# Lower parts of the first weights on VectorE, and the row of ln_mix kept in two accumulators

## The chip, the core and the metric

One core of one Trainium2 chip runs the kernel. The metric is the device time of one execution in microseconds (us), the median of several. TensorE (PE in the rows) multiplies and transposes, VectorE (DVE), ScalarE (ACT) and GpSimd (POOL) work element by element, and the SP queue issues all the transfers between HBM and the on-chip memory SBUF. TensorE writes its results into accumulators (PSUM), which DVE and ACT can read.

## The reference, cut to what matters

The kernel computes one inference step of a decoder layer for 1024 prompt tokens and 32 sample tokens. The change lies in its first lines, the norm of the input and the first columns of the projection:

```
def rmsnorm(x, g):
    xf = x.astype(jnp.float32)
    y = xf * lax.rsqrt(jnp.mean(xf * xf, axis=-1, keepdims=True) + EPS)
    return (y * g.astype(jnp.float32)).astype(x.dtype)
...
    a = rmsnorm(h, ln_mix)
    proj = a @ w_in
    x_m, z_m, o_m, i_pre, f_pre, x_s, z_s = jnp.split(proj, SPLIT_IDX, axis=-1)
```

`h` has 1056 rows of 1024, `ln_mix` is a vector of 1024 and `w_in` is 1024 by 2568. What follows (an S5 scan over `x_s`, a chunkwise mLSTM over `x_m`, output projections, a gated embedding and a last norm) is untouched.

## The kernel before

Every fp32 product is made of three fp32r products: an operand is split into an upper part (`hi`, a cast by ACT) and a lower part (`lo`, the operand minus `hi`), and `mm3` (L122 to L125) multiplies hi by hi, hi by lo and lo by hi. `wtile` (L97 to L117) loads a weight tile, casts `hi` on ACT (L115) and subtracts on the engine that `lo_engine[0]` names (L116). That engine is GpSimd (`G`) for the first six weight tiles: `o00` and `o01` (two halves of the first 264 output-gate columns, `o_w`), and `xs0` to `xs3` (the four 128-column tiles of x_s, `xs_w`). From L932 on it is VectorE for all later ones.

The input comes in nine row tiles of 128 rows, the last of 32 (`x_load`; five buffers). `x_tile(i)` (L151 to L179) normalises one: ACT squares and sums the row (L157; for tile 0 in two halves, L164), DVE and GpSimd make the reciprocal root (L55 and L56; `rsqrt`, the power is GpSimd's), DVE multiplies the row by it and by `ln_row` into `xn` (L159; for tile 0 in two halves, L170), TensorE transposes `xn` in two halves of four blocks (L176, accumulators `tpx`), ACT casts each half into `aTh` (L178) and DVE subtracts for `aTl` (L179). `ln_row` is the vector `ln_mix` repeated on 128 partitions: TensorE multiplies a row of ones by it (L311, two halves, accumulators `tpl`), and DVE copies both halves into SBUF (L312).

The loop at L313 takes tile after tile: load of a tile four ahead, `x_tile`, `o_tile` (24 products of the tile with the output-gate weights, L123 to L125, into `ps_o`; its evacuation is L232 on ACT and L239 on DVE), and after tiles 1, 4 and 8 the x_s columns of a chunk of tiles (`s5_x`, products into `ps_xs`, evacuation L283). Then come the x_s columns of the three other weight tiles, then the S5 stage (its transposes `tpW` on TensorE start at 97.9 us of the span), the mLSTM stage (its transposes `tpxc` from 257.2 us, `tph` to 408.8 us) and the output stages.

The order on each engine up to L933 is made by a scheduler from the program text, data dependences and `tc.high_priority()` blocks; the PE order of the S5 and mLSTM stages is written by hand. Each engine and the SP queue executes its own order strictly, and waits on semaphores. At most eight transfers are under way on the SP queue at a time: there are eight semaphores, and a transfer's issue waits for the landing of the one eight places ahead of it.

Some transposes of small constants stand among the products of the row tiles; one is `tpv` (L920), which needs `scr`, the 24 rows of `state_conv`. `tpc` (L336) needs the small `rows` transfers.

Of the kernel before, what the change touches and what calls it, by code (L numbers as in the profile page):

```python
# [8 lines left out]
F32 = mybir.dt.float32  # L9
# [20 lines left out]
def tile_hymba(ctx: ExitStack, tc: tile.TileContext, d: dict, o: list):  # L30
# [4 lines left out]
    def dma(out, in_):  # L35
        nc.sync.dma_start(out, in_)  # L36
# [46 lines left out]
    def pv(shape, name):  # L83
        return psS.tile(shape, F32, tag="sm", name=name)
# [31 lines left out]
            lo_engine[0].tensor_tensor(lo, raw, hi.bitcast(F32), op=SUB)  # L116
        return hi, lo  # L117

    lo_engine = [G]
    last_mm = [None]  # L120

    def mm3(ps, wh, wl, xh, xl, first, last):  # L122
# [11 lines left out]
    s5c = s5x.enter_context(tc.tile_pool(name="s5c", bufs=1, side="right", reuse_waits="tile"))  # L134
    xphase = ExitStack()
    xp = xphase.enter_context(tc.tile_pool(name="xp", bufs=1, side="right", reuse_waits="tile"))
    ln_row = xp.tile([128, 1024], F32, name="ln_row")

    def x_src(i):
        if i < 8:  # L140
# [3 lines left out]
    def x_load(i):  # L144
        xt = xp.tile([128, 1024], F32, tag="xt", name="xt", bufs=5)
        for q in range(1 if i else 2):
            w = 1024 if i else 512
            dma(xt[:128 if i < 8 else 32, w * q:w * q + w], x_src(i)[:, w * q:w * q + w])
        return xt

    def x_tile(i, xt):  # L151
        n = 128 if i < 8 else 32
        xn = xp.tile([128, 1024], F32, tag="xn", name="xn", bufs=4)
        ss = xp.tile([128, 1], F32, tag="ss", name="ss", bufs=3)
        rr = xp.tile([128, 2], F32, tag="rr", name="rr", bufs=3)
        if i:
            A.activation(xn[:n], xt[:n], AF.Square, accum_out=ss[:n])  # L157
            rsqrt(rr[:n, 1:2], ss[:n], 1.0 / 1024, EPS, rr[:n, 0:1])
            V.scalar_tensor_tensor(xn[:n], xt[:n], rr[:n, 1:2], ln_row[:n], op0=MUL, op1=MUL)  # L159
        else:  # L160

            s2 = xp.tile([128, 2], F32, name="s2")
            for q in range(2):
                A.activation(xn[:, 512 * q:512 * q + 512], xt[:, 512 * q:512 * q + 512], AF.Square,  # L164
                             accum_out=s2[:, q:q + 1])
            V.tensor_scalar(ss, s2[:, 0:1], 1.0 / 1024, EPS, op0=MUL, op1=ADD)
            V.scalar_tensor_tensor(rr[:, 0:1], s2[:, 1:2], 1.0 / 1024, ss, op0=MUL, op1=ADD)
            G.tensor_tensor(rr[:, 1:2], rr[:, 0:1], mhalf[:, 0:1], op=ALU.pow)
            for q in range(2):
                V.scalar_tensor_tensor(xn[:, 512 * q:512 * q + 512], xt[:, 512 * q:512 * q + 512], rr[:, 1:2],  # L170
                                       ln_row[:, 512 * q:512 * q + 512], op0=MUL, op1=MUL)
        c, off = LOC[i]
        for q in range(2):
            tp = pv([128, 4, 128], "tpx")
            for k in range(4):
                T.transpose(tp[:, k, :n], xn[:n, (4 * q + k) * 128:(4 * q + k + 1) * 128], ident[:n, :n])  # L176
            hi = aTh[c][:, 4 * q:4 * q + 4, off:off + n]
            A.copy(hi, tp[:, :, :n])  # L178
            V.tensor_tensor(aTl[c][:, 4 * q:4 * q + 4, off:off + n], tp[:, :, :n], hi.bitcast(F32), op=SUB)  # L179
# [115 lines left out]
    ow = []  # L295
    one_p = xp.tile([1, 128], F32, tag="xn", name="one_p", bufs=4)
    V.memset(one_p, 1.0)
    xts.append(x_load(0))
    ln1 = xp.tile([1, 1024], F32, tag="xn", name="ln1", bufs=4)
    dma(ln1, bcast(d["ln_mix"], 1024, 1))  # L300
    ow.append(o_w(0, 0))
    xts.append(x_load(1))
    ow.append(o_w(0, 1))
# [2 lines left out]
    dma(bgr[:, 0:4], bcast(d["b_igate"], 4))  # L306
    dma(bgr[:, 4:8], bcast(d["b_fgate"], 4))
    xts.append(x_load(3))
    for q in range(2):
        ps = pv([128, 512], "tpl")  # L310
        T.matmul(ps, one_p, ln1[:, 512 * q:512 * q + 512], start=True, stop=True)  # L311
        V.tensor_copy(ln_row[:, 512 * q:512 * q + 512], ps)  # L312
    for i in range(9):  # L313
        if i + 4 < 9:
            xts.append(x_load(i + 4))
# [1360 lines left out]
```

## Time and profile before

| what | value |
|---|---|
| device time, median of 3 runs | 655.43 us (653.66 to 656.03) |
| the profiled execution, its own time | 654.02 us |
| its span, first to last instruction | 652.3 us |
| TensorE busy | 611.8 us, 94% of the span |
| VectorE busy | 456.9 us, 70% |
| ScalarE busy | 255.3 us, 39% |
| GpSimd busy | 102.2 us, 16% |

The span is one execution; what lies around it (654.02 minus 652.3) is 1.7 us. The engines' shares are means over stages with different limits, so what a change to the first stage is worth has to be read from the rows of that stage and of those that take over its results.

### The profile page before, as it was taken

The numbers are of one execution on the slowest core, as the hardware profiler recorded it, in microseconds if no ns is written. First come the engines' busy times: TensorE is split into PE (matmuls) and PEld (weight loads), VectorE is DVE, ScalarE is ACT, GpSimd is POOL, SyncE is SP. The second block draws the span as 40 slices with busy tenths as digits, with TensorE's granted clock in tenths as the row PEclk, the third lists the DMA queues.
The fourth block names the chain that finished last, engine by engine and source line by source line (L and its number), as shares of the span: only waits on it lengthen the run. The fifth ranks groups of instructions, "written<-read, shape, count | busy, mean of one in ns | idle before, by whom it ended". The sixth has DMA issues, their size and how long they took to land.

```text
span 652.3 us, 11603 instructions
## 1 busy us (share of the span) xinstructions
PE 611.8 (94%) x4072; PEld 536.5 (82%) x4072; DVE 456.9 (70%) x1377; ACT 255.3 (39%) x630; POOL 102.2 (16%) x125
## 2 busy tenths in 40 slices
PE   5999999999999997988989897899999999999995
PEld 3999998999999986877968796777888777788885
DVE  5788969999999954998767889964222325566435
ACT  5653743333334555442232335444113225433332
POOL 6840200000000000020201123333001113111001
PEclk9999999999999998997999998999999999999999
DMA  8813353555544438362634655687342274412111
GB/s 265 244 50 56 97 160 95 132 147 156 151 116 111 112 84 275 99 209 88 171 109 114 201 151 164 205 258 219 106 130 86 76 245 141 150 57 98 64 65 65
DMA packets 112417, 90.02 MB, mean 138 GB/s; under 512 B 34080, under 2 KB 94900, under 8 KB 112360
## 3 DMA queue, kind: packets, MB, share of 16 engines
q1 hardware_dynamic: 112360, 89.29, 46.0%
q8 instruction: 32, 0.52, 0.3%
q14 instruction: 25, 0.20, 0.1%
HBM read 61.68 MB, written 27.58 MB: 137 GB/s over the span
## 4 chain that ended last, share of the span: by engine, by line
PE 66%; DMA 12%; DVE 11%; issue 4%; SPq 3%; ACT 2%; POOL 1%; POOLq 0%; DVEq 0%; ACTq 0%
PE po L1495 5%; PE po L1496 5%; PE po L1497 5%; PE po L1604 4%; PE po L1605 4%; PE po L1606 4%; DMA nmb<-d_row 3%; SPq L36 3%; PE ps_xs L123 2%; PE ps_o L123 2%; PE ps_xs L124 2%; PE ps_xs L125 2%; PE ps_o L124 2%; PE ps_o L125 2%; PE ps_xm L123 2%
## 5 line engine op out<-in xcount | busy, mean ns | idle before, releaser
L1604 PE MATMUL po<-wgh,hTh 128*128 128x512 f32 (+1 forms) x136 | 52.1, 383 | 0.0
L1606 PE MATMUL po<-wgh,hTl 128*128 128x512 f32 (+1 forms) x136 | 51.5, 379 | 0.0
L1605 PE MATMUL po<-wgl,hTh 128*128 128x512 f32 (+1 forms) x136 | 51.4, 378 | 0.0
L123 PE MATMUL ps_o<-hi_o,aTh 128*128 128x264 f32 (+2 forms) x136 | 41.0, 301 | 0.0
L123 PE MATMUL ps_zs<-aTh,hi_zs 128*128 128x256 f32 (+2 forms) x96 | 39.9, 415 | 0.0
L125 PE MATMUL ps_o<-hi_o,aTl 128*128 128x264 f32 (+2 forms) x136 | 39.4, 290 | 0.0
L124 PE MATMUL ps_o<-lo_o,aTh 128*128 128x264 f32 (+2 forms) x136 | 39.2, 289 | 0.0
L123 PE MATMUL ps_xm<-aTh,hi_xm 128*128 128x256 f32 (+2 forms) x96 | 34.7, 361 | 0.0
L1299 POOL TENSOR_TENSOR svm<-sv,bmask 96x258 fp32r<-96x258 f32 x16 | 10.1, 633 | 146.5 <-ACT xc L1088 65.9
L1495 PE MATMUL po<-woh,mh 128*128 128x512 f32 x80 | 32.6, 407 | 0.0
L1504 DVE TENSOR_TENSOR hTl<-tr,hTh 128x512 fp32r<-128x512 f32 x16 | 11.1, 691 | 30.6 <-ACT hTh L1503 30.6
L123 PE MATMUL ps_zm<-aTh,hi_zm 128*128 128x256 f32 (+2 forms) x96 | 32.0, 333 | 0.0
L1496 PE MATMUL po<-wol,mh 128*128 128x512 f32 x80 | 31.9, 399 | 0.0
L123 PE MATMUL ps_xs<-aTh,hi_xs 128*128 128x256 f32 (+2 forms) x96 | 31.4, 327 | 0.4 <-ACT xs L287 0.4
L1497 PE MATMUL po<-woh,mlo 128*128 128x512 f32 x80 | 31.7, 396 | 0.0
L125 PE MATMUL ps_zs<-aTh,lo_zs 128*128 128x256 f32 (+2 forms) x96 | 31.6, 329 | 0.0
L124 PE MATMUL ps_zs<-aTl,hi_zs 128*128 128x256 f32 (+2 forms) x96 | 31.5, 328 | 0.0
L124 PE MATMUL ps_xm<-aTl,hi_xm 128*128 128x256 f32 (+2 forms) x96 | 31.3, 326 | 0.0
L125 PE MATMUL ps_xs<-aTh,lo_xs 128*128 128x256 f32 (+2 forms) x96 | 31.3, 326 | 0.0
L124 PE MATMUL ps_xs<-aTl,hi_xs 128*128 128x256 f32 (+2 forms) x96 | 31.3, 326 | 0.0
L125 PE MATMUL ps_xm<-aTh,lo_xm 128*128 128x256 f32 (+2 forms) x96 | 31.2, 325 | 0.0
L125 PE MATMUL ps_zm<-aTh,lo_zm 128*128 128x256 f32 (+2 forms) x96 | 31.0, 323 | 0.0
(594 smaller groups left out, 1907.7 us busy)
## 6 DMA issues: line engine op xcount, KB each, us to landing
xt<-in_x_prompt SPq DMA_DIRECT2D x15, 512.0 KB
Wraw<-in_w_out SPq DMA_DIRECT2D x16, 256.0 KB
Wraw<-in_w_ple_gate SPq DMA_DIRECT2D x16, 256.0 KB
d_h<-xt SPq DMA_DIRECT2D x8, 512.0 KB
h_t<-d_h SPq DMA_DIRECT2D x8, 512.0 KB
out<-g_t SPq DMA_DIRECT2D x14, 256.0 KB
mt<-d_m SPq DMA_DIRECT2D x10, 256.0 KB
d_us<-xs SPq DMA_DIRECT2D x32, 72.0 KB
```

The costliest lines, as they stand in the source:

```text
L36: nc.sync.dma_start(out, in_)
L123: T.matmul(ps, wh, xh, start=first, stop=False)
L124: T.matmul(ps, wh, xl, start=False, stop=False)
L125: last_mm[0] = T.matmul(ps, wl, xh, start=False, stop=last).ins
L1299: G.tensor_tensor(vm[:, :nb], v3.bitcast(F32).unsqueeze(1).to_broadcast([96, nb, 129]), bmask[:, b0:b0 + nb].unsqueeze(2).to_broadcast([96 ...
L1495: T.matmul(ps, mh[:, k % 4, :], hi, start=k == 4, stop=False)
L1496: T.matmul(ps, mh[:, k % 4, :], lo, start=False, stop=False)
L1497: T.matmul(ps, mlo[:, k % 4, :], hi, start=False, stop=k == 3)
L1504: V.tensor_tensor(hTl[i][:, 4 * q:4 * q + 4, :], tp, hi.bitcast(F32), op=SUB)
L1604: T.matmul(ps[:, :b - a], hTh[i][:, k, :], hi[:, ws], start=k == 4, stop=False)
L1605: T.matmul(ps[:, :b - a], hTh[i][:, k, :], lo[:, ws], start=False, stop=False)
L1606: T.matmul(ps[:, :b - a], hTl[i][:, k, :], hi[:, ws], start=False, stop=k == 3)
```

## The change

The lower parts of the first six weight tiles are made by VectorE. The row of `ln_mix` is not copied to SBUF: the two accumulators stay, in another pool (`pn`, two banks that nothing else uses before the S5 stage's `py`, L658, at 115.9 us), and `xn` is made in halves for every tile, each half reading one accumulator. For tile 0 these two instructions have high priority. The load of `ln_mix` is written ahead of that of tile 0.

```
-    lo_engine = [G]
+    lo_engine = [V]
...
-    ln_row = xp.tile([128, 1024], F32, name="ln_row")
...
-            V.scalar_tensor_tensor(xn[:n], xt[:n], rr[:n, 1:2], ln_row[:n], op0=MUL, op1=MUL)
+            for q in range(2):
+                cs = slice(512 * q, 512 * q + 512)
+                V.scalar_tensor_tensor(xn[:n, cs], xt[:n, cs], rr[:n, 1:2], ln_row[q][:n], op0=MUL, op1=MUL)
...
-            for q in range(2):
-                V.scalar_tensor_tensor(xn[:, 512 * q:512 * q + 512], xt[:, 512 * q:512 * q + 512], rr[:, 1:2],
-                                       ln_row[:, 512 * q:512 * q + 512], op0=MUL, op1=MUL)
+            with tc.high_priority():
+                for q in range(2):
+                    V.scalar_tensor_tensor(xn[:, 512 * q:512 * q + 512], xt[:, 512 * q:512 * q + 512], rr[:, 1:2],
+                                           ln_row[q], op0=MUL, op1=MUL)
...
-    xts.append(x_load(0))
     ln1 = xp.tile([1, 1024], F32, tag="xn", name="ln1", bufs=4)
     dma(ln1, bcast(d["ln_mix"], 1024, 1))
+    xts.append(x_load(0))
...
+    ln_row = [pn([128, 512], "tpl") for _ in range(2)]
     for q in range(2):
-        ps = pv([128, 512], "tpl")
-        T.matmul(ps, one_p, ln1[:, 512 * q:512 * q + 512], start=True, stop=True)
-        V.tensor_copy(ln_row[:, 512 * q:512 * q + 512], ps)
+        T.matmul(ln_row[q], one_p, ln1[:, 512 * q:512 * q + 512], start=True, stop=True)
```

Behind these lines the scheduler orders the engines anew. In the rows below, lines of the changed kernel stand one to three higher than those of before (L172 is the tile-0 product of before's L170, L160 is L159, L181 is L179, L922 is L920).

On VectorE, from the end of tile 0's root on, there stood:

```order
L312 COPY ln_row_116<-tpl_161 128x512
L170 SCALAR_TENSOR_TENSOR xn_169<-xt_128,rr_171,ln_row_116 128x512
L312 COPY ln_row_116<-tpl_164 128x512
L55 TENSOR_SCALAR rr_227<-ss_226 128x1
L170 SCALAR_TENSOR_TENSOR xn_169<-xt_128,rr_171,ln_row_116 128x512
L179 TENSOR_TENSOR aTl0_107<-tpx_180,aTh0_104 128x4x128
L159 SCALAR_TENSOR_TENSOR xn_225<-xt_140,rr_227,ln_row_116 128x1024
```

and there stands now (`xn_222` is tile 1's):

```order
L172 SCALAR_TENSOR_TENSOR xn_166<-xt_129,rr_168,tpl_160 128x512
L172 SCALAR_TENSOR_TENSOR xn_166<-xt_129,rr_168,tpl_161 128x512
L116 TENSOR_TENSOR lo_o00_136<-raw_o00_132,hi_o00_135 128x1056
L55 TENSOR_SCALAR rr_224<-ss_223 128x1
L181 TENSOR_TENSOR aTl0_107<-tpx_177,aTh0_104 128x4x128
L160 SCALAR_TENSOR_TENSOR xn_222<-xt_139,rr_224,tpl_160 128x512
L181 TENSOR_TENSOR aTl0_107<-tpx_184,aTh0_104 128x4x128
L160 SCALAR_TENSOR_TENSOR xn_222<-xt_139,rr_224,tpl_161 128x512
L116 TENSOR_TENSOR lo_o01_145<-raw_o01_141,hi_o01_144 128x1056
```

The two copies are gone, tile 0's second half no longer stands behind tile 1's root (L55), and the two lower parts have come in. Next in the new order are the roots of tiles 2 and 3 side by side, so that tile 3's stands ahead of tile 2's `xn` and of tile 1's `aTl`.

On the SP queue, from the weights `xs1` on (`raw_xs` with the lower number; `raw_xs` with the higher one is `xs2`), there stood:

```order
L36 DMA raw_xs_1092<-in_w_in 128x8x128
L36 DMA wq<-in_w_q 128x4x128
L36 DMA wk<-in_w_k 128x4x128
L36 DMA raw_xs_1189<-in_w_in 128x8x128
L36 DMA d_so<-sot 128x256
L36 DMA wv<-in_w_v 128x4x128
L36 DMA scr<-in_state_conv 24x512
```

and there stands now:

```order
L36 DMA raw_xs_1097<-in_w_in 128x8x128
L36 DMA d_so<-sot 128x256
L36 DMA xt<-in_x_sample 32x1024
L36 DMA wq<-in_w_q 128x4x128
L36 DMA wk<-in_w_k 128x4x128
L36 DMA wv<-in_w_v 128x4x128
L36 DMA scr<-in_state_conv 24x512
L36 DMA d_so<-sot 128x256
L36 DMA raw_xs_1194<-in_w_in 128x8x128
```

The load of `xs2` and the store of tile 1's gates have moved from ahead of `scr` to behind it; the load of tile 8 and the store of tile 0's gates, which stood ahead of `xs1`, stand behind it now.

On TensorE, at the transposes of `scr` among the products of tile 3 (accumulator `ps_o_379` in both), there stood:

```order
L125 MATMUL ps_o_379<-hi_o00_136,aTl1_108 128x264
L176 MATMUL tpx_417<-ident_60,xn_410 128x128 x4
L920 MATMUL tpv_1393<-ident_60,scr_1391 128x24 x4
L123 MATMUL ps_o_379<-hi_o01_145,aTh1_105 128x264
L124 MATMUL ps_o_379<-lo_o01_146,aTh1_105 128x264
```

and there stands now:

```order
L178 MATMUL tpx_372<-ident_60,xn_357 128x128 x4
L123 MATMUL ps_o_379<-hi_o00_135,aTh1_105 128x264
L124 MATMUL ps_o_379<-lo_o00_136,aTh1_105 128x264
L922 MATMUL tpv_1398<-ident_60,scr_1396 128x24 x4
L125 MATMUL ps_o_379<-hi_o00_135,aTl1_108 128x264
```

The transposes of `scr` have moved ahead by ten of tile 3's products and four transposes.

## Rows read from the trace of the kernel before

**Rows 1.** The page, part 1: busy us, share of the span, instructions, by engine.

```profile
PE 611.8 (94%) x4072; PEld 536.5 (82%) x4072; DVE 456.9 (70%) x1377; ACT 255.3 (39%) x630; POOL 102.2 (16%) x125
```

**Rows 2.** Waits of PE, whole span: total us, times, longest us.

```profile
PE tpx L176 <- DVE xn L170: 2.5, 1, 2.5
...
PE tpv L920 <- DMA scr<-in_state_conv: 1.0, 1, 1.0
```

**Rows 3.** Timeline of 5 to 15 us: start, us, engine, line, idle before.

```profile
5.02 3.75 PE L311 MATMUL tpl<-ln,one_p 1*128 1x512 f32 x4 [5.02 <-DMA ln<-in_ln_mix]
...
8.17 1.08 ACT L115 CAST hi_o<-raw_o 128x1056 fp32r<-128x1056 f32 x1 [2.99 <-DMA raw_o<-in_w_in]
...
10.42 0.57 ACT L178 CAST aTh<-tpx 128x512 fp32r<-128x512 f32 x1
...
10.63 1.66 DVE L170 SCALAR_TENSOR_TENSOR xn<-xt,rr,ln_row 128x512 f32<-128x512 f32 x1
...
12.67 2.43 POOL L116 TENSOR_TENSOR lo_o<-raw_o,hi_o 128x1056 fp32r<-128x1056 f32 x1
12.81 3.38 DVE L159 SCALAR_TENSOR_TENSOR xn<-xt,rr,ln_row 128x1024 f32<-128x1024 f32 x1
...
13.11 0.57 PE L123 MATMUL ps_o<-hi_o,aTh 128*128 128x264 f32 x1
...
13.69 0.42 PE L125 MATMUL ps_o<-hi_o,aTl 128*128 128x264 f32 x1
...
14.92 1.06 ACT L157 ACTIVATE xn<-xt 128x1024 f32<-128x1024 f32 x1 [0.84 <-DMA xt<-in_x_prompt]
```

**Rows 4.** Timeline of 15 to 25 us, the same columns.

```profile
15.67 0.42 PE L125 MATMUL ps_o<-hi_o,aTl 128*128 128x264 f32 x1
...
18.12 0.68 DVE L179 TENSOR_TENSOR aTl<-tpx,aTh 128x512 fp32r<-128x512 f32 x1
...
18.32 0.28 PE L123 MATMUL ps_o<-hi_o,aTh 128*128 128x264 f32 x1
...
19.30 0.28 PE L125 MATMUL ps_o<-hi_o,aTl 128*128 128x264 f32 x1
...
19.77 0.29 PE L125 MATMUL ps_o<-hi_o,aTl 128*128 128x264 f32 x1
...
24.14 0.36 PE L125 MATMUL ps_xs<-aTh,lo_xs 128*128 128x256 f32 x1
```

**Rows 5.** Groups of DVE by form, whole span: busy us, mean ns, idle before.

```profile
L1592 DVE SCALAR_TENSOR_TENSOR e_t<-pe,sc,lnp 128x512 f32<-128x512 f32 x16 | 11.3, 746 | 6.0 <-POOL sc L56 6.0
L159 DVE SCALAR_TENSOR_TENSOR xn<-xt,rr,ln_row 128x1024 f32<-128x1024 f32 x7 | 11.1, 1579 | 0.3 <-POOL rr L56 0.3
...
L116 DVE TENSOR_TENSOR lo_zm<-raw_zm,hi_zm 128x1024 fp32r<-128x1024 f32 x4 | 4.8, 1208 | 0.0
```

**Rows 6.** Timeline of 23 to 34 us: the SP queue's issues and PE.

```profile
24.25 1.83 SPq L36 DMA_DIRECT2D raw_xs<-in_w_in  x1
...
29.41 0.47 SPq L36 DMA_DIRECT2D scr<-in_state_conv  x1
...
30.34 0.29 PE L124 MATMUL ps_o<-lo_o,aTh 128*128 128x264 f32 x1
...
33.29 0.42 PE L920 MATMUL tpv<-ident,scr 24*128 24x24 f32 x4 [1.01 <-DMA scr<-in_state_conv]
```

**Rows 7.** Window 23 to 33.3 us: busy us by engine, PEclk, DMA share, GB/s.

```profile
23.00:33.30 10.30, 9.29 (x79) 8.94 (x77) 7.82 (x14) 6.42 (x12) 10.30 (x9) 1.00 0.81 228
```

**Rows 8.** Timeline of 76 to 88 us.

```profile
78.13 1.05 ACT L115 CAST hi_xs<-raw_xs 128x1024 fp32r<-128x1024 f32 x1
...
79.50 2.48 DVE L411 TENSOR_TENSOR cu<-rBi,bas_r 128x128 f32<-128x128 f32 x1
...
87.78 0.09 DVE L276 MEMSET xs<- 128x32 f32 x1 [5.48 <-DMA d_us<-xs]
```

**Rows 9.** Window 296 to 300 us, the columns of rows 7.

```profile
296.00:300.00 4.00, 3.25 (x12) 2.01 (x11) 4.00 (x9) 0.00 (x0) 0.00 (x0) 0.50 0.05 20
```

## The prediction

> **What bounds the kernel now.** I read the page first: TensorE is busy for 94% of the span [rows 1], so a change can win only where TensorE waits, or runs at the lower of its clocks. The table of TensorE's waits comes next, and from it the two that this change can reach: 2.5 us at tile 0's transposes, which wait for `xn`, and 1.0 us at the transposes of `scr`, which wait for a transfer [rows 2]. Then the timeline of the first 34 us. The first real product starts only at 13.11 us [rows 3]. [...] From there TensorE runs product upon product. So what the change is worth is the lead that TensorE has over its old timeline from 18 us on, and how much of it survives to the end.
>
> **Tile 0.** `ln_mix` landed at 5.02 us and its four passes took 3.75 us [rows 3]. It is now issued one transfer earlier (an issue takes 0.47 us [rows 6]), so the halves of the row are in their accumulators at about 6.4 and 8.3 us. The two copies fall away, and tile 0's second half no longer stands behind tile 1's root, where it ended at 10.63 + 1.66 = 12.29 us [rows 3]. No row has this product with the row in an accumulator; the nearest, with another operand in one, takes 746 ns [rows 5]. I take that: `xn` is ready at 7.1 and 9.1 us, the second half 3.2 us earlier. TensorE does not get all of it. ACT casts the first half of `aTh` at 10.42 us, behind `hi_o` (raw weights at 8.17 us) and the square of tile 1, and that order stays; the cast ends at 10.99 us [rows 3]. DVE makes `lo_o00` between 9.3 and 10.5 us (1208 ns [rows 5]), before it is asked for. So the first product starts at 11.05 us instead of 13.11, its third operand `aTl` is there at 11.7, and ten more at 0.22 us and eight transposes bring TensorE to tile 0's second half at about 16.2 us. Tile 0 ends near 17.5 us, against 19.30 + 0.28. **Lead: 2.0 us.** [...]
>
> **Tile 1.** It needs its `aTl`, and DVE's new order puts the root of tile 3 ahead of it. Tile 3 lands at 14.92 us as before, since the transfers ahead of it are the same bytes, and ACT's square takes 1.06 [rows 3]. So DVE waits to 16.1 us, does two halves of tile 2's `xn` (1.3 us), then `aTl` (0.68 us [rows 4]): ready at 18.2 instead of 18.80. TensorE's product that needs it starts at 18.25 instead of 19.77 [rows 4]. **Lead: 1.5 us.** DVE goes on with tile 3's `xn`, tile 1's second `aTl` (20.2), tile 4's `xn` (21.7) and only then `lo_xs0`, to 22.9 us. TensorE wants it at about 22.2. Before, the product with `lo_xs` stood at 24.14 us [rows 4], behind four transposes (0.35 us) that now come after it: 22.9 against 23.8. **Lead: 0.9 us.**
>
> **Lower parts as work.** Six subtractions of 1.21 us come to DVE, 7.3 us. Two copies go (some 0.7 us each, as `aTl`, the other pass of 512 columns out of an accumulator [rows 4]), and the split costs 2 x 746 less the whole row's time. That is 1579 ns in the mean of seven, but one of these took 3.38 us while GpSimd made a lower part [rows 3]; the other six give (11.1 - 3.38) / 6 = 1.28 us [rows 5], so 0.21 us a tile, 1.7 us for eight. DVE gets back 2.1 us there, 0.9 us of the 1.66, and 2.2 us of the 2.48 that a small product took beside `lo_xs3` [rows 8]. In sum some 2 us more work on DVE up to 80 us, hidden by the 5.48 us for which it idles at 87.78 us before a memset that waits for the store of `xs1` [rows 8]. One part of this moves badly: `lo_xs3` waits on DVE's own queue for ACT's cast, 78.13 + 1.05 = 79.18 us, with 17 small products of 3.7 us behind it. They end at 79.2 + 1.2 + 3.7 = 84.1 us, 3.7 us ahead of the memset, so it costs nothing. Without that cover it would cost 1.8 us (84.1 less the 82.3 at which DVE arrived before).
>
> [...]
>
> **The transfer of `scr`.** This is where I expect the lead to go. Before, TensorE waited 1.01 us for it, to 33.29 us [rows 6]. Its transposes now stand earlier by ten products (0.12 us) and four transposes (0.35 us): 1.6 us. At equal lead they are equal at 33.29 - 1.6 = 31.7 us, and TensorE reaches them at 29.6. In the new SP order `scr` passes `xs2` (512 KB) and a store (128 KB). From 23 us to its landing the engines moved 228 GB/s at a share of 0.81 [rows 7]; 0.655 MB are 2.9 us, which gives a landing at 30.4 us. But tile 7's load and the loads behind it move down: their issues wait for a landing eight places ahead, and tile 6's load now stands behind that of tile 5, which I put at 18.0 us. I get 1 to 2.3 us of delay for the stream behind, so `scr` lands between 30.4 and 32.7 us and the lead is between 1.3 (cut to DVE's 0.9) and -1.0 us. Nothing settles which; I take 31.2 us. **Lead: 0.5 us.**
>
> [...]
>
> **From 34 us on.** TensorE is full to the S5 stage, and DVE's start into that stage follows the store of `xs1`, which follows TensorE; both shift by the lead. In the mLSTM stage the scheduler swapped a few instructions on DVE (same instructions, other order), where DVE is full, so I count nothing, with one reservation below.
>
> **Sum.** 654.02 - 0.5 = 653.5 us for such an execution. The profiled one lies 1.4 us below the median of 655.43, so I predict 655.43 - 0.5 = **654.9 us**.
>
> **Rivals.**
> - *The whole lead arrives* (25%): `scr` lands in time, DVE keeps up, and the 2.0 us of tile 0 and the 1.0 us of the `scr` wait both stay. Against it stand the root of tile 3 and `lo_xs0`. 655.43 - 3.0 = 652.4 us. It becomes "faster" with 0.3 us more, for instance if a stretch at the lower clock in the mLSTM stage goes: half of them.
> - *Nothing arrives* (20%): `scr` lands at 32 us or later, because tile 7 delays the stream. For it: the transfers wait for landings eight places ahead. 655.4 to 656.4 us.
> - *Slower, by the clock* (7%): TensorE's granted clock is 0.50 between 296 and 300 us [rows 9], the 1.2 GHz level, after a wait for DVE, and DVE's order just there is changed. If the swap leaves TensorE idle once more, another such stretch of 4 us with TensorE busy costs 2 us, two of them 4. Against it: the first set of normalised rows moves ahead in DVE's new order, which shortens that idle time. It decides from two more stretches on: 655.43 + 4.0 - 0.5 = 658.9 us.
> - *The forecast* (48%): a lead of 0 to 1.3 us, 654.1 to 655.4 us.
>
> **How the numbers follow.** A measurement of this kernel tells about 0.5%, 3.3 us, from no change. Faster is half of the first rival, 0.13. Slower is most of the clock's, 0.06. The rest, 0.81, is the same. The range goes from the first rival with one clock stretch gone (652.4 - 0.6 = 651.8; the rest of it is left out) to the top of the second, 656.4, with 0.8 us for one stretch at the lower clock more, which TensorE fills in part: 657.2.
>
> **What would show it.** Right: first product at about 11 us; no `xn` of 3 us; a wait of TensorE for `aTl` at tile 1 and one for `lo_xs` near 22 us; the longest wait of the first 50 us at `tpv`, 1 to 2.5 us; DVE's wait before the memset at 87 us shorter, 3 to 4 us; the S5 stage's transposes about 0.5 us earlier than before. Wrong: no wait at `tpv` (then 2 us or more are won), the memset without idle time before it (then DVE is the bound and up to 1.8 us are lost), or another number of stretches at 0.50.

## The result and the profile after

The changed kernel takes **660.08 us** in the median of 5 runs (659.02 to 661.47), the kernel before 655.43 in the median of 5 (653.66 to 656.40). The ratio is **1.0067, with an interval of 1.0043 to 1.0092**: 4.4 us slower. The ratio and its interval are estimated from all the executions, and differ a little from the quotient of the two medians; what is priced in us below is taken from the ratios. The forecast was 654.9 with a range of 651.8 to 657.2, so time and sign were both wrong.

The profiled execution of the changed kernel spans 657.9 us; its own time is 660.08, so 2.2 us lie around the span, where there were 1.7. Part 1 of its page:

```profile
PE 616.1 (94%) x4072; PEld 539.5 (82%) x4072; DVE 454.0 (69%) x1389; ACT 255.4 (39%) x630; POOL 83.9 (13%) x119
```

TensorE has the same 4072 instructions [rows 1] and is busy 4.3 us longer. TensorE's waits of the first 100 us (total, times, longest), where [rows 2] were the ones to beat:

```profile
PE tpl L314 <- DMA ln<-in_ln_mix: 3.5, 1, 3.5
PE ps_o L123 <- ACT aTh L180: 2.1, 2, 1.8
PE tpv L922 <- DMA scr<-in_state_conv: 1.3, 1, 1.3
PE ps_o L125 <- DVE aTl L181: 0.2, 1, 0.2
PE tpx L178 <- DVE xn L172: 0.2, 1, 0.2
PE ps_xs L125 <- DVE lo_xs L116: 0.2, 1, 0.2
```

The timeline at the places that [rows 3, 4, 8] showed, the first product, the first one with `lo_xs`, and the memset behind the store of `xs1`:

```profile
11.17 0.59 PE L123 MATMUL ps_o<-hi_o,aTh 128*128 128x264 f32 x1 [1.79 <-ACT aTh L180]
...
22.36 0.39 PE L125 MATMUL ps_xs<-aTh,lo_xs 128*128 128x256 f32 x1 [0.15 <-DVE lo_xs L116]
...
86.98 0.09 DVE L278 MEMSET xs<- 128x32 f32 x1 [3.67 <-DMA d_us<-xs]
```

Up to here the change did what was forecast: first product at 11.17 us (11.05), `lo_xs` in time within 0.15 us, the memset's idle time down from 5.48 to 3.67 us (3 to 4). The loss is later. It shows when each product's start is set against the start of the same product in the profiled execution of before. The table gives the median difference of all products of 5 us from the time named, for all kernels whose first stage is of one kind or the other (the experiments e1 to e15 follow below):

| execution | first product at | from 20 us | 100 us | 230 us | 310 us | 640 us |
|---|---|---|---|---|---|---|
| before, profiled | 13.11 | 0 | 0 | 0 | 0 | 0 |
| e2, first stage of before | 12.21 | -1.56 | -1.88 | -1.14 | +3.34 | +4.79 |
| e9, first stage of before | 12.03 | -1.87 | -2.16 | +2.68 | +3.92 | +7.44 |
| e13, first stage of before | 12.30 | -1.59 | -1.89 | +2.40 | +3.48 | +3.26 |
| **changed** | 11.17 | -1.76 | -0.72 | +1.80 | +5.07 | +5.61 |
| e1, changed | 11.17 | -1.47 | -0.14 | +2.30 | +2.30 | +2.66 |
| e8, changed | 10.74 | -2.38 | +1.08 | +1.12 | +3.04 | +5.96 |
| e15, changed | 10.99 | -1.48 | -0.39 | -0.25 | -0.82 | -0.75 |

Three things are to be seen. The changed kernel still leads the profiled execution by 0.72 us at 100 us, but that execution was a late one there: three others with the same first stage are 1.9 to 2.2 us earlier. Between 100 and 230 us 2.5 us are lost, and between 230 and 310 us 3.3 more. One row is one execution, and its last column is no price: the profiled executions of e8 and e9 are the longest of their twelve, that of e15 is the shortest.

**The S5 stage.** On the SP queue one transfer changed its place: the store of zeros into `dK` (`dK<-zt`, 256 KB, L539 before) stood ahead of the eight stores `d_us0` and four loads `cn`, and stands behind them now. The scheduler chose that place, and no run shows why: the memset that makes the zeros ends ahead of the first `d_us0` store in both. The SP queue's issues of before from 58 us on, and then those of the changed kernel:

```profile
59.07 3.10 SPq L36 DMA_DIRECT2D cn<-in_s_C_re  x4
62.58 0.62 SPq L36 DMA_DIRECT2D dK<-zt  x1
65.80 0.61 SPq L36 DMA_DIRECT2D d_us<-xs  x1
```

```profile
59.62 2.93 SPq L36 DMA_DIRECT2D cn<-in_s_C_re  x4
65.98 5.45 SPq L36 DMA_DIRECT2D d_us<-xs  x8
71.53 2.64 SPq L36 DMA_DIRECT2D cn<-in_s_C_im  x4
74.28 0.60 SPq L36 DMA_DIRECT2D dK<-zt  x1
```

Some 120 us later the S5 stage stores `ks` into the same `dK` and loads it back as `tz`, eight times. The load is issued when the store has landed: for the seventh pair the last update of the store's semaphore comes at 196.19 us in before and the load at 196.21, in the changed kernel at 198.15 and 198.17. In every kernel seven of the pairs take 2.4 to 4.5 us from store to load, wherever the zeros stand; only the seventh differs (the expectations below count from 0 and call it the sixth). This seventh pair in before, and behind it the row of VectorE that waits for a store which stands behind the load on the queue:

```profile
192.33 0.53 SPq L36 DMA_DIRECT2D dK<-ks  x1
...
196.21 0.61 SPq L36 DMA_DIRECT2D tz<-dK  x1
...
201.37 0.42 DVE L671 SCALAR_TENSOR_TENSOR y<-sq,py 128x256 f32<-128x256 f32 x1 [0.42 <-DMA d_y<-y]
```

and in the changed kernel, with the wait of TensorE that follows:

```profile
192.50 0.53 SPq L36 DMA_DIRECT2D dK<-ks  x1
...
198.17 0.60 SPq L36 DMA_DIRECT2D tz<-dK  x1
...
203.21 0.42 DVE L673 SCALAR_TENSOR_TENSOR y<-sq,py 128x256 f32<-128x256 f32 x1 [2.07 <-DMA d_y<-y]
...
219.12 0.44 PE L123 MATMUL ps_zm<-aTh,hi_zm 128*128 128x384 f32 x1 [1.25 <-ACT zc L723]
```

The store was issued 0.17 us later and the load 1.96: **5.7 us from store to load instead of 3.9**. Everything behind the load on the queue is late, VectorE waits 2.07 us, and TensorE 1.25 us at 219 us. That is 1.5 of the 2.5 us which this stage loses in the changed kernel's profile. The other 0.9 us go earlier, at a wait of TensorE for VectorE's `xs_`, 0.41 us in before. e2, whose zeros stand ahead, waits there as long (the changed kernel, then e2), so this part is not the store's:

```profile
195.57 0.47 PE L665 MATMUL py<-xs__2765,cs 128*128 128x136 f32 x2 [1.34 <-DVE xs__2765 L655]
```

```profile
194.40 0.47 PE L663 MATMUL py<-xs__2760,cs 128*128 128x136 f32 x2 [1.33 <-DVE xs__2760 L653]
```

**The mLSTM stage.** The scheduler put a stretch of 85 instructions on VectorE, 16 on ScalarE and 10 on SP into another order around 276 to 300 us. The row of `Cst` there in before:

```profile
280.63 0.33 DVE L1178 SCALAR_TENSOR_TENSOR Cst<-Cst,dcb,nu 128x129 f32<-128x129 f32 x1
```

and in the changed kernel, VectorE, with ScalarE's pass that it waits for:

```profile
282.15 1.24 ACT L1090 ACTIVATE xc<-xm,hcols 128x1024 f32<-128x1024 f32 x1 [1.05 <-DMA xm<-d_xm]
...
283.42 1.28 DVE L1092 SCALAR_TENSOR_TENSOR xc<-xm,hcols,xc 128x1024 f32<-128x1024 f32 x1 [1.46 <-ACT xc L1090]
...
285.12 0.34 DVE L1180 SCALAR_TENSOR_TENSOR Cst<-Cst,dcb,nu 128x129 f32<-128x129 f32 x1
```

The first tap of the next head's convolution (L1092) now stands ahead of `Cst` (L1180), the state that TensorE multiplies next, and of the rows behind it. VectorE waits 1.46 us for it, then works 1.28 us, and only then makes `Cst`. From 270 to 310 us TensorE's waits, all for rows of VectorE, sum to 7.1 us in the changed kernel and to 5.3 in e1, which has the old order (4.1 against 3.1 us of them for `qd`). The granted clock of four stretches in the changed kernel (columns as in [rows 7]):

```profile
259.40:262.80 3.40, 3.40 (x16) 3.31 (x15) 3.20 (x8) 1.73 (x5) 0.00 (x0) 0.50 0.50 187
279.90:283.30 3.40, 3.40 (x18) 3.40 (x18) 2.06 (x12) 1.38 (x2) 0.07 (x1) 0.50 0.46 170
300.40:307.20 6.80, 5.26 (x20) 4.49 (x21) 4.95 (x12) 0.72 (x1) 0.00 (x0) 0.50 0.42 124
419.90:423.30 3.40, 3.40 (x15) 3.12 (x16) 3.32 (x9) 1.48 (x3) 0.00 (x0) 0.51 0.66 203
```

and of the stretches of before up to there, with the one where the changed kernel has a new one:

```profile
257.00:260.40 3.40, 3.24 (x13) 3.15 (x14) 2.69 (x8) 2.35 (x7) 0.00 (x0) 0.50 0.84 313
279.00:283.00 4.00, 4.00 (x26) 3.28 (x25) 4.00 (x19) 2.21 (x4) 0.64 (x1) 1.00 0.55 173
294.50:301.30 6.80, 5.90 (x20) 4.36 (x21) 6.32 (x18) 0.27 (x1) 0.01 (x1) 0.50 0.21 66
403.80:407.20 3.40, 3.32 (x16) 3.03 (x15) 3.40 (x15) 0.97 (x2) 0.00 (x0) 0.50 0.29 99
```

There is one stretch more at a granted clock of 0.50, of 3.4 us, at 279.9 us. Half of full speed for 3.4 us can cost at most 1.7 us (my estimate from the 0.50, with TensorE at work for all of it), so it and the longer waits share the 3.3 us. It does not belong to the new order: e3, e5, e6, e8 to e10 and e12 to e14, all with the old one, have such a stretch between 276.8 and 285.7 us too. e12's:

```profile
276.80:280.20 3.40, 3.40 (x18) 3.40 (x18) 2.75 (x14) 1.81 (x3) 0.56 (x1) 0.50 0.49 179
```

### The profile page after: what moved, and what is told of

Its sections match the earlier page's. It is cut to its first block, busy times and chain, and to the rows that moved or that the text cites. A ratio compares the mean times of both kernels' runs of the same rounds, so it can differ in the third digit from the quotient of the medians.

```text
span 657.9 us, 11609 instructions
## 1 busy us (share of the span) xinstructions
PE 616.1 (94%) x4072; PEld 539.5 (82%) x4072; DVE 454.0 (69%) x1389; ACT 255.4 (39%) x630; POOL 83.9 (13%) x119
## 4 chain that ended last, share of the span: by engine, by line
PE 65%; DMA 13%; DVE 11%; SPq 3%; issue 3%; ACT 3%; POOL 0%; POOLq 0%; DVEq 0%; ACTq 0%
PE po L1497 5%; PE po L1498 5%; PE po L1499 5%; PE po L1606 3%; PE po L1607 3%; PE po L1608 3%; SPq L36 3%; DMA nmb<-d_row 3%; PE ps_o L123 2%; PE ps_o L125 2%; PE ps_o L124 2%; PE ps_xm L123 2%; PE ps_xs L123 2%; PE ps_xs L124 2%; PE ps_xs L125 2%
## 5 line engine op out<-in xcount | busy, mean ns | idle before, releaser
L125 PE MATMUL ps_zs<-aTh,lo_zs 128*128 128x256 f32 (+2 forms) x96 | 31.5, 328 | 0.0
L123 PE MATMUL ps_xs<-aTh,hi_xs 128*128 128x256 f32 (+2 forms) x96 | 31.2, 325 | 0.0
L124 PE MATMUL ps_zm<-aTl,hi_zm 128*128 128x256 f32 (+2 forms) x96 | 31.0, 323 | 0.0
```

Of the source, the lines that this page charges most:

```text
L123: T.matmul(ps, wh, xh, start=first, stop=False)
L124: T.matmul(ps, wh, xl, start=False, stop=False)
L125: last_mm[0] = T.matmul(ps, wl, xh, start=False, stop=last).ins
```

## The experiments

Many of them set the order of instructions by hand. At the end of the program a list of names makes each instruction follow the one ahead of it on its engine, with no wait added:

```
+    for row in order:
+        for m, n in zip(row, row[1:]):
+            tc.add_manual_dep(at[n], m, mybir.DependencyInfo(
+                mybir.DependencyClass.NoSync, mybir.DependencyReason.DATA), reason="order")
```

Every time below is a median, beside that of the kernel before on the same chip; the ratio behind it, with its interval, is that of all the executions (for e3 1.0022, where the medians alone would give 1.0038).

**e1, the changed kernel with the mLSTM stage in its old order** (the list holds the 85, 16 and 10 instructions that had been swapped).

> The changed kernel, with the 85 VectorE, 16 ScalarE and 10 SP instructions around 276 to 300 us put back into the order that they had before; its first 100 us are those of the changed kernel. Theory ORDER: the other order that the scheduler chose in the mLSTM stage costs what TensorE's offset grew there, from +1.36 to +5.07 us, so this kernel takes 660.1 - 3.7 = 656.4 us. Theory PHASE: the loss there is that of transfers and waits that came at another time because everything ahead was shifted, whatever the order: 660 us. In either case TensorE's lead at the first transposes of the S5 stage is 0.7 us, as in the changed kernel. On the 2.5 us lost in the S5 stage: if they belong to the first 100 us of the changed kernel, they are lost here again between 155 and 220 us; if they are chance of one execution, 0 to 2.5 us.

659.04 us against 656.28, ratio 1.0050 (1.0025 to 1.0076). TensorE loses nothing between 230 and 310 us (+2.30 in both columns), and 1.1 us come back (1.0067 - 1.0050, the intervals overlap, so that this pair does not tell 1.1 from nothing). Most of the loss stays.

**e2, the kernel before with the mLSTM stage in the changed order** (the same list, the other way round).

> The kernel before, with the same VectorE, ScalarE and SP instructions around 276 to 300 us in the order of the changed kernel, and nothing else changed. Theory ORDER: 655.4 + 3.7 = 659.1 us, with VectorE waiting some 1.5 us for the convolution's first pass (ScalarE) near 282 us and TensorE's waits for the normalised rows longer by 2 us and more. Theory PHASE: 655.4 us, within 1 us, and no loss between 276 and 310 us.

657.88 against 656.28, 1.0018 (0.9995 to 1.0042). In its profile the loss is larger than in the changed kernel, 4.5 us, from -1.14 at 230 us to +3.34 at 310, and VectorE waits at the same tap:

```profile
281.16 1.28 DVE L1090 SCALAR_TENSOR_TENSOR xc<-xm,hcols,xc 128x1024 f32<-128x1024 f32 x1 [0.89 <-ACT xc L1088]
```

So that order alone makes the loss there, but the ratio shows 1.2 us of it, with an interval that just holds none.

**e3 and e4, either half of the change alone.** e3 keeps the row in the accumulators and makes the lower parts on GpSimd; its store of zeros stands ahead of the `d_us0` stores. e4 is the kernel before with the lower parts on VectorE; its store of zeros stands behind them.

```
-    lo_engine = [V]      # e3, from the changed kernel
+    lo_engine = [G]
-    lo_engine = [G]      # e4, from the kernel before
+    lo_engine = [V]
```

> The changed kernel with the six lower parts left to GpSimd; the row stays in the two accumulators. Its order from the S5 stage on is that of the kernel before on all engines. Theory ORDER: no loss in the mLSTM stage, so 655.4 us less the lead that is left at the S5 stage, 0 to 2 us: 653.4 to 655.4. Theory PHASE: anywhere from 655 to 660 us, with the losses at 160 to 220 and 276 to 300 us as in the changed kernel if its lead is the same.

> The kernel before with the six lower parts on VectorE and nothing else. Theory ORDER: the first half of the swapped VectorE order (the convolution's pass ahead of two accumulators' evacuation) is not there, so no 3.7 us are lost near 280 us; the time is 655.4 us within 1.5. A rival, that VectorE's 7.3 us of added work are what costs: 657 us and more, with the loss already there at the S5 stage's first transposes.

e3: 658.78 against 656.28, 1.0022 (0.9998 to 1.0045). e4: 660.13, 1.0071 (1.0046 to 1.0096). By the times alone the loss of the whole change would come with the lower parts. But e4 loses it in part at other places. TensorE waits longer for `aTh` in the first stage,

```profile
PE ps_o L123 <- ACT aTh L178: 3.7, 3, 1.4
```

and stands at +1.80 us at 20 us, where the changed kernel has -1.76. From +1.82 at 100 us it goes to +4.80 at 230, but not by the path of the changed kernel: the 3 us are gone by 200 us, before the late load can act (201.52 us), in a wait for VectorE and a stretch at a granted clock of 0.50 behind it, and there is no wait of TensorE at 219 us:

```profile
198.70 0.47 PE L663 MATMUL py<-xs__2760,cs 128*128 128x136 f32 x2 [1.92 <-DVE xs__2760 L653]
```

```profile
199.10:202.50 3.40, 3.40 (x16) 3.37 (x15) 3.40 (x10) 1.14 (x7) 0.10 (x1) 0.50 0.00 0
```

So it is in part luck that e4 and the whole change lose the same, and e3's interval leaves room for a loss of 3 us by the row alone. What the two runs do show is the store: store to load of the seventh `dK` takes 5.7 us in e4, 3.7 in e3.

**e5, e6, e7, whether VectorE's longer stream of instructions is to blame.** e5 is the kernel before, its order held, with 14 more memsets ahead. e6 is e1 with 23 small memsets given to GpSimd, so VectorE has fewer instructions. e7 gives four of the six lower parts back to GpSimd.

```
-    V.memset(one_p, 1.0)                # e5, from the kernel before
+    for _ in range(15):
+        V.memset(one_p, 1.0)
-    V.memset(zt, 0.0)                   # e6, here and in ten other lines, from e1
+    G.memset(zt, 0.0)
+    lo_engine[0] = G                    # e7, ahead of xs_w(0), from the changed kernel
```

> The kernel before, in its own order on every engine, with 14 more VectorE memsets of 1 x 128 in its first microseconds, where VectorE is idle; they write again what the first one wrote. Theory STREAM: the three kernels with the lower parts on VectorE share 12 to 17 more VectorE instructions, 2.2 us instead of 1.7 around the span, and 5.4 to 5.7 us instead of 3.2 to 3.9 from the sixth store of dK in the S5 stage to the load behind it; if the longer instruction stream is the reason, this kernel shows both, and takes 656.3 + 0.45 + 2 = 658.7 us. Theory WORK: the loss belongs to the lower parts themselves (their time on VectorE, and what they move): 656.3 us within 0.7, and 1.7 us around the span.

> The changed kernel with the mLSTM stage in the old order (as in the first experiment, 659.0 us), and 23 small memsets that VectorE made moved to GpSimd, so that VectorE's instruction stream is shorter than before the change (1580 instructions against 1591); the order of everything else is the same. Theory STREAM: 1.7 us around the span, 3.2 to 3.9 us for the sixth store of dK, and 659.0 - 2.5 = 656.5 us. Theory WORK: 659.0 us within 0.7, 2.2 us around the span or some value between.

> The changed kernel with only the two lower parts of the output-gate weights on VectorE, those that stand before the first products; the four of xs are GpSimd's again. VectorE's stream has 1601 instructions, and its order in the mLSTM stage is in part the changed one. Theory STREAM: 2.2 us around the span and 5.5 us for the sixth store of dK, as with all six: 659 to 660 us. Theory WORK: two of six subtractions, so a third of the 3.3 to 4.7 us that six cost, and the lead of the first products kept: 656.3 us plus 0 to 2.

e5: 656.48 against 656.13, 1.0013 (0.9996 to 1.0031), 0.3 us lost in the S5 stage (-0.45 to -0.17). e6: 658.19 against 656.13, 1.0050 (1.0025 to 1.0076), the S5 loss is there in full (+1.19 to +4.04, store to load 5.4 us). The length of the stream is not the cause. What e6 did change is the time around the span: 1.7 us, as before, against 2.2 in e1, so 0.45 us of the change's loss lie there. e7: 662.16 against 656.13, 1.0088 (1.0056 to 1.0120), the longest of the three; its mLSTM order is a third one (+2.72 at 230 us, +6.70 at 310) and it settles nothing about the lower parts.

**e8 and e9, the store of zeros put back, and moved alone.** e8 is e1 with that one transfer ahead of the `d_us0` stores again. e9 is the kernel before with it behind them and behind the second four loads `cn`, every other instruction in its old place. On SP, in e9:

```
-dK<-zt
 d_us0<-xs x8
 cn<-in_s5_C_im x4
+dK<-zt
```

> The kernel of the first experiment (changed, old order in the mLSTM stage), with one transfer moved on the SP queue: the store of zeros into dK (62.6 us of the span before the change, 74.3 us after it) stands ahead of the eight stores of xs0 and four loads again, as before the change. Nothing else differs. Theory ZEROS: in the kernels whose zero store stands behind (the changed one and experiments 1, 4 and 6) the sixth store of dK took 5.4 to 5.7 us to the load behind it, in those where it stands ahead (before, 2, 3, 5, 7) 3.2 to 4.2; if that place is the reason, this kernel shows 3.2 to 4.2 us and some 2.3 us less in the S5 stage: 656.7 us. Theory LOWER: the place of that store is only a companion of the xs lower parts on VectorE, which are the reason in a way not yet seen: 5.5 us, and 659.0 us as in the first experiment.

> The kernel before, in its own order on all engines, with only that store of zeros into dK moved behind the eight stores of xs0 and the four loads, where the changed kernel has it. Theory ZEROS: the sixth store of dK takes 5.4 to 5.7 us, and the time is 656.2 + 2.3 = 658.5 us. Theory LOWER: 3.2 to 4.2 us there, and 656.2 us within 0.7.

e8: **655.77 against 655.87, 1.0008** (0.9987 to 1.0029). e9: **658.31, 1.0036** (1.0016 to 1.0056). One transfer's place costs 2.4 us in the kernel before and brings back 2.8 in the changed one (1.0050 - 1.0008). e9's rows of the S5 stage, first the store of zeros:

```profile
71.96 0.60 SPq L36 DMA_DIRECT2D dK<-zt  x1
...
191.28 0.53 SPq L36 DMA_DIRECT2D dK<-ks  x1
...
196.84 0.61 SPq L36 DMA_DIRECT2D tz<-dK  x1
...
202.79 0.42 DVE L671 SCALAR_TENSOR_TENSOR y<-sq,py 128x256 f32<-128x256 f32 x1 [2.89 <-DMA d_y<-y]
...
218.69 0.44 PE L123 MATMUL ps_zm<-aTh,hi_zm 128*128 128x384 f32 x1 [2.07 <-ACT zc L721]
```

They are the rows of the changed kernel again: 5.6 us from store to load, then VectorE's wait, then TensorE's. In e9 a stretch at the lower clock stands right behind TensorE's wait, as it does in e13 (from 219.4 us); the changed kernel and e1 have none there:

```profile
220.10:223.50 3.40, 3.40 (x13) 3.40 (x12) 3.40 (x7) 2.80 (x9) 0.00 (x0) 0.50 0.47 110
```

So part of the 4.8 us that e9's profile loses from 100 to 230 us is clock. The profiled execution of e8 (660.43) loses nothing on that path (+1.08 to +1.12), where e1 lost 2.4.

**e13, e14, e15, what it is about that place.** e13 is the kernel before with the store of zeros behind the eight `d_us0` stores, but ahead of the four loads `cn`; e14 has it further ahead instead, in front of the loads `Br`, `Bi` and the first four `cn`; e15 is e1 with that store on ScalarE's queue.

```
-dK<-zt                    # e13, SP
 d_us0<-xs x8
+dK<-zt
 cn<-in_s5_C_im x4
+dK<-zt                    # e14, SP
 Br, Bi, cn<-in_s5_C_re x4
-dK<-zt
-    dma(dK[:, 0:16, :, 0:128].rearrange("u r i x -> u (r i) x"), zt)                  # e15
+    nc.scalar.dma_start(dK[:, 0:16, :, 0:128].rearrange("u r i x -> u (r i) x"), zt)
```

> The kernel before with the store of zeros (dK from zt, 256 KB) moved only half as far back as in the run that cost 2.4 us: behind the eight stores d_us0, still ahead of the four loads cn. Theory STORES (what costs the time is that the eight small stores d_us0 go ahead of it): as with the full move, 658 to 658.5 us, and the sixth store dK of the S5 stage takes 5.4 us or more to the load tz that follows it. Theory LOADS (it is the four loads cn that must not go ahead): as the kernel before, 655.8 us within 0.5, and that store takes 4.2 us or less. A time half between them would say that each place counts for itself.

> The kernel before with the store of zeros moved six transfers ahead, in front of the loads Br, Bi and the first four cn. Theory GRADE (the earlier the better, since the store is then further from the S5 stage): at least 0.5 us less than 655.8. Theory SIDE (only whether it is ahead of or behind the d_us0 stores and the second cn loads counts): 655.8 within 0.5 us, the sixth store dK at 4.2 us or less.

> The changed kernel with the mLSTM stage in the order of before and the store of zeros issued by ScalarE on its own queue instead of SyncE's. Theory PLACE (its place among the transfers of SyncE's queue is what costs): about the 655.8 us of the run with the store put ahead, sixth store dK at 4.2 us or less. Rival TIME (that it moves its bytes late, near 70 us, is what costs, on whichever queue): 658.5 to 659 us as without the edit, sixth store dK at 5.4 us or more.

e13: 657.45 against 655.54, 1.0026 (1.0003 to 1.0049), store to load 5.5 us, the waits of e9 again. It is the eight stores that must not go ahead. e15: 656.79 against 655.54, 1.0019 (0.9997 to 1.0042), and its S5 stage has neither wait, with 3.35 us from store to load:

```profile
63.55 1.17 ACTq L541 DMA_DIRECT2D dK<-zt  x1
...
192.26 0.53 SPq L36 DMA_DIRECT2D dK<-ks  x1
...
195.61 0.61 SPq L36 DMA_DIRECT2D tz<-dK  x1
```

ScalarE issued the store at 63.55 us, about where it stood before, so e15 shows that it need not be on SP's queue, but not whether the time at which the bytes move matters too. e14: **660.62 against 655.54, 1.0066** (1.0041 to 1.0091), where no theory had a loss. Its seventh pair takes 4.2 us, so for the S5 stage only the side counts; but the store, now ahead of `Br` on SP, waits there for its memset to 62.25 us, and everything behind it waits as well, down to TensorE:

```profile
PE tpC L505 <- DMA cn<-in_s_C_re: 3.2, 1, 3.2
```

**e10, e11, e12, the changed kernel with all of this put back.** e10 is e6 with the store of zeros ahead and the load of `scr` issued ahead of that of `xs1`; e11 is e10 with the mLSTM stage in the changed order; e12 is the kernel before with only the load of `scr` moved.

```
+scr<-in_state_conv        # SP, e10 and e12
 raw_xs1<-in_w_in
-scr<-in_state_conv
```

> The changed kernel with what the experiments so far point to: the old order in the mLSTM stage, 23 small memsets on GpSimd (1.7 us around the span instead of 2.2), the zero store of dK ahead as in experiment 8, and the load of scr ahead of that of xs1, so that TensorE's wait for it (1.3 us in the changed kernel, followed by a stretch at the lower clock in experiments 6 and 7) goes. If all count: lead at the S5 stage 1 to 2 us over the profiled kernel before, S5 stage as before, 656.2 - 1 = 655.2 us. If the zero store is not the reason: 657.5 us. If the wait for scr only moves to the loads of wq and wk: 656.5 us.

> The combined kernel of the last call (lower parts on VectorE, small memsets on GpSimd, the store of zeros and the load of scr put ahead, mLSTM stage in the order of before) with one thing altered: the mLSTM stage stands in the order of the change. Theory ORDER (that order costs time by itself, because VectorE then stands at the first tap of head 3's convolution while ScalarE has not made it): 1.2 us (what the pair of medians of the first call gave) to 3.6 us (what the profile of that run lost from 270 to 310 us) more than the combined kernel's 654.23, so 655.4 to 657.8 us; VectorE waits about 1.5 us for ScalarE near 280 us, and TensorE loses 2.5 us or more there against the combined kernel. Rival CLOCK (the order costs nothing in the mean; the stretches of lower granted clock only fall elsewhere): 654.2 us within 0.7, and TensorE's loss near 280 us is taken back by 420 us.

> The kernel before with one transfer moved on SyncE's queue: the load of scr is issued ahead of the load of xs1. Theory SCR (what the combined kernel has over the kernel before is TensorE's wait for scr, 1.0 us before and 1.3 us after, and the change itself brings nothing): 655.9 less 0.7 to 1.0, so 654.9 to 655.2 us, and no wait of TensorE for scr. Rival LEAD (the combined kernel's 1.6 us come from the lower parts made earlier): the same as before, 655.9 us within 0.5, since the transfer moved ahead delays xs1 by what it saves.

e10: **654.23 against 655.87, 0.9977** (0.9958 to 0.9995), faster than both kernels. e12: 654.67 against 655.83, 0.9988 (0.9969 to 1.0007), with no wait for `scr` left in its first 100 us. e10 is ahead of e12 by 0.0011 of the time, 0.7 us, which these intervals (1.2 us either way, each) don't tell from nothing: what the change brings by itself, after every mend, lies somewhere between 1 us lost and 2.4 us won. e11: 657.34 against 655.83, 1.0025 (0.9999 to 1.0051), so 0.0048 or 3.1 us more than e10, and these two intervals lie apart. VectorE's wait is where it was (1.64 us at 282.16), and the window of 270 to 310 us (columns as in [rows 7]) in e11 and then e10 tells it from the clock:

```profile
270.00:310.00 40.00, 32.59 (x200) 27.79 (x199) 32.31 (x121) 13.19 (x32) 5.48 (x6) 0.87 0.43 135
```

```profile
270.00:310.00 40.00, 35.15 (x225) 30.49 (x224) 34.52 (x129) 13.97 (x33) 5.33 (x7) 0.87 0.43 134
```

Both had the same mean clock there, 0.87, and e11's TensorE was busy 2.6 us less and did 25 instructions fewer; its waits sum to 7.5 us against 4.9. The loss is the wait, not the clock, and it is not taken back: e11 stands 3.6 us behind e10 at 310 us (+3.85 against +0.21) and 5.2 behind at 640.

## Why the prediction was wrong

**The step that failed** is "From 34 us on": that TensorE is full to the S5 stage, that both engines shift by the lead, and that the swap in the mLSTM stage counts nothing. Both later stages have their own waits, and the new order of instructions reached into both. Beside it the lead of the first stage was wrong by its reference.

- *The S5 stage*, counted at nothing. The runs give 1.7 us (e13), 2.4 (e9) in the kernel before and 2.0 (e1 to e15), 2.8 (e1 to e8) in the changed one. Of these the 2.0 alone is not clear of nothing. I had followed the SP queue only as far as `scr`; the store of zeros that moved past twelve transfers was in the same order. But even with it in view I would have counted the bytes and found no reason in them.
- *The mLSTM stage*, "(same instructions, other order), where DVE is full, so I count nothing". The tap was put ahead of the state that TensorE's products need, and waits for ScalarE: 1.1 us from the changed kernel to e1, 1.2 in e2, 3.1 from e10 to e11. Only the last is clear of nothing by its intervals, and these are wide enough to hold the other two. My rival there priced a stretch at the lower clock; the changed kernel has one more, which kernels with the old order have too, but e10 and e11 show the wait to cost the time at an equal clock. Of the level that the rival names the traces show the granted 0.50, with products of 416 columns 0.35 us apart in the stretch of [rows 9], 1.2 columns a ns, against 0.18 to 0.19 us behind it at 1.00; no run shows a frequency.
- *Around the span* 0.45 us (2.2 against 1.7), which I had taken as fixed. It goes with the lower parts' move (e4 has all of it, e3 0.2 us), and e6 has the 1.7 again. In the trace of the changed kernel a second block of 8 KB of instructions is fetched behind the last instruction, to 1.37 us after it, where before has one fetch there, to 0.68 us; that this is the cause is not shown.
- *The first stage.* Its steps held: the first product, the wait for `aTh` that limits it, `lo_xs`, and `scr`, where 1.3 us of waiting ate the lead. TensorE's wait for `scr` ended at 31.19 us; I had taken a landing at 31.2, out of 30.4 to 32.7 with nothing to decide, so that it fell there is luck. The sum for tile 0 counts 0.22 and later 0.12 us for a product of 264 columns: these are the steps of [rows 3, 4] (13.69 to 15.67 us, 18.32 to 19.30 us), both at a granted clock of 1.00, and the changed kernel has them too, 0.22 us from 12.28 us and 0.12 from 17.21, at 1.00 from 11 to 23 us. Why they differ no run shows. The sum for VectorE was off, to no harm: some 2 us more work were forecast, and its busy time fell by 2.9 us (456.9 to 454.0).
- *The reference of the first stage* is what failed there. The lead was counted against one execution, in which TensorE had waited for `scr` to 33.29 us; in e2, e9 and e13, with the same code up to there, that wait ended at 31.39, 30.90 and 31.06. The prediction's own sum, in which the transposes stand 1.6 us earlier now, makes of these a lead of -1.4 to -1.9 us in place of +0.5. The four with before's first stage differ by 2.2 us at 100 us. Against their mean (-1.48) the changed ones (-0.72, -0.14, +1.08, -0.39, mean -0.04) are 1.4 us late, not 0.5 early. At 20 us they were still 0.5 ahead, -1.77 against -1.26. Between the two TensorE waits for transfers: 1.7 us for `scr` in e15 and 1.9 in e8, there with a stretch at the lower clock behind it (0.50 from 32.8 to 36.2 us), where e2, e9 and e13 wait 0.7, 0.5 and 0.4; e1 has no such wait, but one of 1.1 us for `aTh` at 30.65 us. A fifth execution of before's code up to 57 us, e14, waits 1.0 us for `scr` and stands at -0.33 at 35 us, so that code comes late in some executions too. The outcome is that of my rival "Nothing arrives", which I had put behind the forecast, but not by its condition: in no changed execution of the table did the transposes of `scr` start later than 31.5 us, and the rival asked for 32. e10 and e12, where the load of `scr` goes first, have no wait for it.

The sum of the pieces: taken off the changed kernel one after another (1.1 by e1, 2.8 by e8, 0.5 left) they add up to 4.4 us whatever they are, so that is no test. Put into the kernel before one by one they are a test: the store's place 2.4 (e9), the mLSTM order 1.2 (e2) and around the span 0.45 make 4.0 us against 4.4, with 1.3 to 1.5 us either way on each of the first two.

The clock does not carry these differences. Within a kernel the longer executions have the lower mean granted clock (e14: 657.87 us at 0.981, 664.06 at 0.971), by my estimate, from a line through the executions of all the experiments, 3.8 us for 0.01. But the means of the kernels that are compared lie close: e9 0.981 and before beside it 0.982, e8 0.982, e10 0.983 and e11 0.981. By that line 0.3 us of e9's 2.4 and 0.7 of the 3.1 between e10 and e11 go with the clock, at most.

The price of the halves held. Their row in the changed kernel (shortest, median and longest ns, first and last start):

```profile
L160 DVE SCALAR_TENSOR_TENSOR xn<-xt,rr,tpl x16: 729/740/748, 11.8 to 39.7; 128x512 f32<-128x512 f32 x14, 32x512 f32<-32x512 f32 x2
```

I had taken 746 ns. None is stretched as the 3.38 us of [rows 3] were. In this kernel the lower parts have gone from GpSimd at the same time, but e3 parts the two: it has the row in the accumulators and the lower parts on GpSimd, and its 16 halves take 729 to 749 ns, with a lower part beside eight of them:

```profile
27.92 2.38 POOL L116 TENSOR_TENSOR lo_xs<-raw_xs,hi_xs 128x1024 fp32r<-128x1024 f32 x1
27.99 1.41 DVE L160 SCALAR_TENSOR_TENSOR xn<-xt,rr,tpl 128x512 f32<-128x512 f32 x2 [0.35 <-POOL rr L56]
```

So with the row in an accumulator a half takes 729 to 749 ns, GpSimd's lower part beside it or not, where with both inputs in SBUF the whole row took 3.38 us beside one [rows 3].

**What stays open** is why the place of a store at 62 to 74 us delays the landing of another at 195. The two are in one tensor and on one queue. The packets of the seventh store have ended by 194.9 us in before and by 195.1 in the changed kernel, 2.5 to 2.6 us after the store, and only the last of its semaphore's updates are late: they come at 194.67, 194.76, 194.87 and 196.19 us in before, at 194.86, 194.93, 196.49 and 198.15 in the changed kernel. In the changed kernel the DMA engines then stand idle for the 3 us up to the load:

```profile
195.10:198.10 3.00, 2.53 (x19) 2.56 (x20) 2.94 (x9) 1.17 (x5) 0.10 (x1) 1.00 0.00 0
```

No run here shows for which write these late updates wait, nor why the order of the transfers 120 us before should choose it. Also open is what the mLSTM order costs in the changed kernel itself: 1.1 us in one pair and 3.1 in another are, by their intervals, not shown to differ.

## What to carry to other kernels

An edit that shifts work between engines gives a scheduler new due times, and what it reorders can lie far behind the edit. Compare the orders of all engines and queues over the whole program, and look above all for a pass put ahead of the producer that the bounding engine waits for, and for transfers that changed sides. Both can be held in place by hand, as e8 and e10 do. A lead of half a microsecond can't be read against one profiled execution: set it against two or three of the same code first.

## What the runs showed that I had not expected

- The seventh store `dK<-ks` takes 3.0 to 4.2 us to the load behind it when the store of zeros stood ahead of the eight `d_us0` stores or on another queue (e8, e10, e15: 3.6, 3.0, 3.35), and 5.4 to 5.7 us when it stood behind them on SP (the changed kernel, e1, e4, e6, e9, e13).
- Executions with the same instructions in the first stage start the S5 stage up to 2.2 us apart (0 against -2.16).
- A transfer set six places further ahead cost 4.3 us (e14, 1.0066), since it waits on the queue for its source and holds up the loads behind it; its mean clock is lower too (0.978 against 0.981), so by the estimate above some 1.3 us of this may be clock.
